# An encoder layer in which two FFN heads and the last tile are put in written order

## The chip, the cores and the metric

The kernel runs on one core of a Trainium2 chip. The metric is device time in microseconds (us) of one execution. The engines named below are TensorE (PE in the rows; its weight loads are PEld), VectorE (DVE), ScalarE (ACT), GpSimd (POOL) and SyncE (SP). Each takes its instructions in order, from a queue of its own, and waits where the next one's inputs or buffers are not ready.

## The reference

One layer of a bidirectional encoder, width 1024, on 512 columns (two sequences of 256 tokens): half an FFN, a mixer of two branches, half an FFN.

```python
def swiglu(h, w_in, w_out):
    a, g = jnp.split(h @ w_in, [D_FF], axis=-1)          # D_FF = 2816
    return (jax.nn.silu(a) * g) @ w_out
...
    x = x + 0.5 * swiglu(rmsnorm(x, g_ffn1), w_ffn1_in, w_ffn1_out)
    h = rmsnorm(x, g_mix)
...
    o_a = gla_mixer(gla_q, gla_k, gla_v, gla_r, gla_lr, gla_w2_fwd, gla_b2_fwd, gla_w2_bwd, gla_b2_bwd, gla_norm)
    o_b = mlstm_mixer(ml_qk, ml_v, ml_o, ml_if, ml_conv_w, ml_conv_b, ml_b_if, ml_norm)
    merged = jax.nn.sigmoid(gate_a.astype(f32)) * o_a + jax.nn.sigmoid(gate_b.astype(f32)) * o_b
    x = x + merged.astype(x.dtype) @ w_out
    x = x + 0.5 * swiglu(rmsnorm(x, g_ffn2), w_ffn2_in, w_ffn2_out)
```

gla_mixer is a gated linear attention in both directions, with per-column decays that are summed up along the sequence; mlstm_mixer the same with scalar gates and a running maximum.

## The kernel before

x is held transposed in eight tiles of 128 x 512. Every fp32 product is made of three matmuls over split operands: high times high, high times low, low times high (names end in h and l, or hi and lo). A weight tile is loaded raw, ScalarE casts its high part, and the low part is made in one of two ways: VectorE subtracts (split2), or ScalarE writes the negated high part and a GpSimd DMA adds the raw weights to it from memory (split_dma: names wal, wbl).

An FFN begins with its **head**. first_tiles does six column tiles (ps_f1i, three a/g pairs) as x comes in, tile by tile; in the first FFN that is the start of the kernel. rms_stat makes the scale r of the norm; its matmuls are st and sp, and dg is the diagonal between. x_sums then makes, in four steps (bodies 0 to 3), the sums and differences of x tiles from which the later products are built: u, v, t, w in VectorE, four casts xch in ScalarE, four xcl in VectorE. Two pairs are done as **plain** tiles (w_plain: names f1p and f1p2, here called the first and the second plain tile, each with two banks). The remaining pairs (f1s, numbered from 5) are done in pair, by seven products of 12 matmuls of 256 columns each, over two weight buffers: a new tile's wah waits until the tile before the last has let its buffer go. gated and activate apply r, silu and the gate, and split the result for the second matrix (out_tile).

The second FFN (f2) runs the same code; its last output tile is done in last2, in two halves of 256 columns, each with its own sum of squares (sql), scale and stores.

The order of all this is set by a scheduler, but for what is marked as high priority. The mixer between comes in gla_half (vg, gA, gB, ops_g), twice, and the mLSTM gate rows (gF, gN, gR) between the two calls.

## Time and profile before

| what | value |
|---|---|
| median of 3 runs | 1207.36 us (1204.89 to 1208.26) |
| the profiled execution | 1207.96 us |
| its span in the trace | 1206.2 us |
| busy, TensorE / VectorE / ScalarE / GpSimd | 98% / 61% / 50% / 10% |
| mean DMA rate | 118 GB/s |

The times in rows count from the span's start. What lies between the span and the execution's time, 1.8 us, is outside the trace. Matmuls overlap, so the busy time of one is longer than its turn.

### The profile page before, as it was taken

What the parts mean: (1) busy time and instruction counts of PE and PEld (TensorE: products, weight loads), DVE (VectorE), ACT (ScalarE), POOL (GpSimd) and SP (SyncE); (2) the same over time, 40 slices, a digit from 0 to 9 for tenths busy, and PEclk for the clock granted to TensorE, in tenths of its full rate; (3) what the DMA queues carried; (4) which work ended last, traced back from release to release, by engine and by line L of the source; (5) the groups of instructions that cost most, each with busy time, mean ns of one, the idle gap of its engine ahead of it and who ended that gap; (6) DMA issues with size and microseconds to landing.
All of it is one profiled execution on the core that took longest, in us unless ns stands there. A gap on an engine that the chain in (4) does not pass through costs nothing.

```text
span 1206.2 us, 16870 instructions
## 1 busy us (share of the span) xinstructions
PE 1177.4 (98%) x6651; PEld 1019.8 (85%) x6651; DVE 736.0 (61%) x1127; ACT 609.0 (50%) x989; POOL 114.9 (10%) x130
## 2 busy tenths in 40 slices
PE   8999999999999998999999999999989999999996
PEld 6798899899987887888888888888879899989985
DVE  6974576567547888657573453463585467566643
ACT  6753365256536655575762332244555256336541
POOL 4100000000021004020000000013100000000011
PEclk9999999999999999999999999999989999999997
DMA  7853555356414214232253223232754356446512
GB/s 236 192 137 112 130 141 139 116 132 164 125 53 127 88 37 131 71 105 70 79 184 114 91 93 114 81 94 44 184 141 130 101 134 156 132 119 154 139 46 70
DMA packets 57952, 141.88 MB, mean 118 GB/s; under 512 B 5320, under 2 KB 19656, under 8 KB 57872
## 3 DMA queue, kind: packets, MB, share of 16 engines
q1 hardware_dynamic: 47904, 110.38, 29.4%
q0 software_dynamic: 8160, 28.06, 13.4%
q10 hardware_dynamic: 1808, 2.36, 0.6%
q8 instruction: 52, 0.85, 0.3%
q14 instruction: 28, 0.23, 0.1%
HBM read 135.51 MB, written 2.11 MB: 114 GB/s over the span
## 4 chain that ended last, share of the span: by engine, by line
PE 89%; DVE 5%; DMA 2%; issue 2%; ACT 1%; SPq 1%; POOL 0%; POOLq 0%; DVEq 0%
PE psy_f L318 16%; PE psq_f L318 8%; PE psz_f L318 4%; PE ps_f1o L203 3%; PE ps_f1o L204 3%; PE ps_f1o L202 3%; PE ps_f2o L203 3%; PE ps_f2o L202 3%; PE ps_f2o L204 3%; PE ps_f2i L258 3%; PE pt_ga L545 2%; PE pt_ga L543 2%; PE pt_ga L544 2%; PE pt_gb L545 2%; PE pt_gb L543 2%; PE pt_gb L544 2%
## 5 line engine op out<-in xcount | busy, mean ns | idle before, releaser
L318 PE MATMUL psy_f<-xch_f,wal_f1s 128*128 128x256 f32 x204 | 57.3, 281 | 0.0
L318 PE MATMUL psy_f<-xcl_f,wah_f1s 128*128 128x256 f32 x204 | 57.2, 281 | 0.0
L318 PE MATMUL psy_f<-xch_f,wah_f2s 128*128 128x256 f32 x204 | 57.2, 281 | 0.0
L318 PE MATMUL psy_f<-xcl_f,wah_f2s 128*128 128x256 f32 x204 | 57.2, 281 | 0.0
L318 PE MATMUL psy_f<-xch_f,wal_f2s 128*128 128x256 f32 x204 | 57.2, 280 | 0.0
L318 PE MATMUL psy_f<-xch_f,wah_f1s 128*128 128x256 f32 x204 | 57.2, 281 | 0.0
L543 PE MATMUL pt_ga<-whi_ga,xh_m 128*128 128x512 f32 x128 | 50.7, 396 | 0.0
L545 PE MATMUL pt_ga<-whi_ga,xl_m 128*128 128x512 f32 x128 | 50.7, 396 | 0.0
L545 PE MATMUL pt_gb<-whi_gb,xl_m 128*128 128x512 f32 x128 | 50.5, 396 | 0.0
L544 PE MATMUL pt_ga<-wlo_ga,xh_m 128*128 128x512 f32 x128 | 50.4, 394 | 0.0
L543 PE MATMUL pt_gb<-whi_gb,xh_m 128*128 128x512 f32 x128 | 50.4, 394 | 0.0
L544 PE MATMUL pt_gb<-wlo_gb,xh_m 128*128 128x512 f32 x128 | 50.4, 394 | 0.0
L94 DVE TENSOR_TENSOR wlo_ga<-raw_ga,whi_ga 128x1024 fp32r<-128x1024 f32 x16 | 19.6, 1224 | 46.0 <-ACT whi_ga L93 46.0
L404 DVE SCALAR_TENSOR_TENSOR x<-ps_f2o,x 128x512 f32<-128x512 f32 x23 | 15.8, 689 | 41.6 <-PE ps_f2o L204 41.6
L93 ACT CAST whi_gb<-raw_gb 128x1024 fp32r<-128x1024 f32 x16 | 16.8, 1048 | 45.7 <-PE pt_ga L545 29.5
L94 DVE TENSOR_TENSOR wlo_gb<-raw_gb,whi_gb 128x1024 fp32r<-128x1024 f32 x16 | 19.6, 1222 | 32.7 <-ACT whi_gb L93 32.6
L318 PEld LDWEIGHTS psy_f<-xch_f,wah_f1s 128*128 128x128 f32 x204 | 38.4, 189 | 0.1
L318 PEld LDWEIGHTS psy_f<-xcl_f,wah_f2s 128*128 128x128 f32 x204 | 38.4, 188 | 0.1
L318 PEld LDWEIGHTS psy_f<-xcl_f,wah_f1s 128*128 128x128 f32 x204 | 38.4, 188 | 0.1
L318 PEld LDWEIGHTS psy_f<-xch_f,wal_f1s 128*128 128x128 f32 x204 | 38.5, 189 | 0.0
L318 PEld LDWEIGHTS psy_f<-xch_f,wah_f2s 128*128 128x128 f32 x204 | 38.3, 188 | 0.1
L318 PEld LDWEIGHTS psy_f<-xch_f,wal_f2s 128*128 128x128 f32 x204 | 38.4, 188 | 0.0
(1155 smaller groups left out, 4039.1 us busy)
## 6 DMA issues: line engine op xcount, KB each, us to landing
raw_f1s<-in_w_f SPq DMA_DIRECT2D x17, 512.0 KB, 3.7
wal_f1s<-in_w_f POOLq DMA_DIRECT2D x17, 512.0 KB, 5.5
raw_f2s<-in_w_f SPq DMA_DIRECT2D x17, 512.0 KB, 3.7
wal_f2s<-in_w_f POOLq DMA_DIRECT2D x17, 512.0 KB, 5.7
raw_ga<-in_w_tm SPq DMA_DIRECT2D x16, 512.0 KB, 3.6
raw_gb<-in_w_tm SPq DMA_DIRECT2D x16, 512.0 KB, 3.6
sum_f1s<-in_w_f SPq DMA_DIRECT2D x17, 256.0 KB, 3.3
raw_f1s<-in_w_f SPq DMA_DIRECT2D x17, 256.0 KB, 4.0
```

The lines of the kernel that those rows point to most:

```text
L93: nc.scalar.copy(hi[:, :width], raw[:, :width])
L94: nc.vector.tensor_tensor(out=lo[:, :width], in0=raw[:, :width], in1=hi.bitcast(F32)[:, :width], op=ALU.subtract)
L202: nc.tensor.matmul(ps, lhsT=wh, rhs=xh, start=start, stop=False)
L203: nc.tensor.matmul(ps, lhsT=wh, rhs=xl, start=False, stop=False)
L204: nc.tensor.matmul(ps, lhsT=wl, rhs=xh, start=False, stop=stop)
L258: nc.tensor.matmul(pss[m], lhsT=w[:, f[m]], rhs=xp, start=k == n == 0, stop=k == KD - 1 and n == 2)
L318: nc.tensor.matmul(ps, lhsT=l[:, f], rhs=m, start=start and k == n == 0, stop=stop and k == 3 and n == 2, skip_group_check=True)
L404: nc.vector.scalar_tensor_tensor(out=x[i], in0=ps, scalar=0.5, in1=x[i], op0=ALU.mult, op1=ALU.add)
L543: nc.tensor.matmul(pss[t], lhsT=xh, rhs=hi[:, ws], start=k == 0, stop=False)
L544: nc.tensor.matmul(pss[t], lhsT=xh, rhs=lo[:, ws], start=False, stop=False)
L545: nc.tensor.matmul(pss[t], lhsT=xl, rhs=hi[:, ws], start=False, stop=k == KD - 1)
```

## The change

There are four parts. At the start the first raw weights come in two halves over the queues of ScalarE and SyncE, and the parameters pt by ScalarE's queue instead of GpSimd's; the first xh is made by VectorE; a ScalarE activation stands early; there are 14 warm matmuls for 10. The head of each FFN gets a block in which VectorE and ScalarE keep the order of the code; the code in it is rearranged, and tile 0's split is cut in two. The second call of gla_half moves ahead of the scans of the mLSTM gates. last2 gets a written order on TensorE, VectorE and ScalarE. rms_cols and spread are each cut into two functions (rms_sum and diag, broadcast) with the same instructions; that part of the diff is left out.

```diff
@@ -117,15 +117,20 @@
     NF = 6
     raw1 = [(w_raw, w_sum)[kp % 2](f"first{kp}").rearrange("p a b -> p (a b)").rearrange("p (i m f) -> p i m f", i=2, m=NF)
             for kp in range(4)]
-    nc.scalar.dma_start(x[0], xT[0:P, :])
-    nc.gpsimd.dma_start(pt, par)
     for k in range(KD):
-        if k:
-            nc.sync.dma_start(x[k], xT[k * P:(k + 1) * P, :])
-        nc.sync.dma_start(raw1[k // 2][:, k % 2], w_f1[0:NF, :, k * P:(k + 1) * P].rearrange("m p f -> p m f"))
+        nc.sync.dma_start(x[k], xT[k * P:(k + 1) * P, :])
+        for n in ((range(0, 3), range(3, NF)) if k == 0 else (range(NF),)):
+            (nc.scalar if k == n[0] == 0 else nc.sync).dma_start(
+                raw1[k // 2][:, k % 2, n[0]:n[-1] + 1],
+                w_f1[n[0]:n[-1] + 1, :, k * P:(k + 1) * P].rearrange("m p f -> p m f"))
+        if k == 0:
+            nc.scalar.dma_start(pt, par)
+
+    act0 = cp.tile([P, 1], F32, name="act0")
+    nc.scalar.activation(act0, ones[:, 0:1], AF.Copy, scale=2.0)
 
     warm = scp("warm", (P, P))
-    for _ in range(10):
+    for _ in range(14):
         nc.tensor.matmul(warm, lhsT=ones, rhs=ones, start=True, stop=True)
     eps = cp.tile([P, 1], F32, name="eps")
     nc.gpsimd.memset(eps, EPS)
...
@@ -184,7 +199,10 @@
     def split_x(k, gcol, sq, name):
         hi = slab(f"xh_{name}{k}", F32R)
         lo = slab(f"xl_{name}{k}", F32R)
-        nc.scalar.activation(hi, x[k], AF.Copy, scale=col(gcol + k))
+        if name == "a" and k == 0:
+            nc.vector.tensor_scalar(out=hi, in0=x[k], scalar1=col(gcol + k), scalar2=None, op0=ALU.mult)
+        else:
+            nc.scalar.activation(hi, x[k], AF.Copy, scale=col(gcol + k))
         nc.vector.scalar_tensor_tensor(out=lo, in0=x[k], scalar=col(gcol + k), in1=hi.bitcast(F32),
                                        op0=ALU.mult, op1=ALU.subtract)
         add_sq(k, sq, name)
@@ -242,7 +260,10 @@
                 whi, wlo = (t.rearrange("p a b -> p (a b)")[:, i * NF * P:(i + 1) * NF * P]
                             for t in wide) if kp else (t.rearrange("p a b -> p (a b)")[:, :NF * P]
                                                        for t in w_pair("wb", 2, f"{name}{k}"))
-                if kp < dma_from:
+                if k == 0:
+                    for h in (slice(0, 3 * P), slice(3 * P, NF * P)):
+                        split2(whi[:, h], wlo[:, h], raw[:, i, h])
+                elif kp < dma_from:
                     split2(whi, wlo, raw[:, i])
                 else:
                     split_dma(whi, wlo, raw[:, i], raw[:, i])
@@ -432,9 +453,6 @@
             nc.vector.tensor_tensor(out=g, in0=b, in1=r, op=ALU.mult)
             act_of[j] = t, g
 
-        def act(j):
-            act_of[j] = activate(*act_of[j], f"{name}{j}")
-
         def plain(pss, w):
             for ps, (hi, lo) in zip(pss, w):
                 for k in range(KD):
@@ -443,25 +461,29 @@
 
         top = NP - 1
         steps = x_sums(gcol, r, name)
-        for _ in range(3):
+        with tc.manual_schedule(engines={nc.vector.engine, nc.scalar.engine}):
             next(steps)
-        w_p = w_plain(w_a, NP, f"{name}p")
-        next(steps)
-        gated(top, pss[2 * top], pss[2 * top + 1])
-        xc += next(steps)
-        plain(banks[0], w_p)
-        w_p = w_plain(w_a, NP + 1, f"{name}p2")
-        gated(0, pss[0], pss[1])
-        nxt = units[0][0]()
-        banks.append([acc(f"ps_{name}p{n}", True) for n in range(2, 4)])
-        plain(banks[1], w_p)
-        gated(1, pss[2], pss[3])
-        for j in range(NP):
-            act(j)
-        for j in (NP, NP + 1):
-            gated(j, *banks[j - NP])
-            act(j)
-        hs += [act_of[j] for j in range(NP + 2)]
+            next(steps)
+            w_p = w_plain(w_a, NP, f"{name}p")
+            next(steps)
+            next(steps)
+            gated(top, pss[2 * top], pss[2 * top + 1])
+            w_p2 = w_plain(w_a, NP + 1, f"{name}p2")
+            xc += next(steps)
+            gated(0, pss[0], pss[1])
+            plain(banks[0], w_p)
+            nxt = units[0][0]()
+            gated(1, pss[2], pss[3])
+            banks.append([acc(f"ps_{name}p{n}", True) for n in range(2, 4)])
+            plain(banks[1], w_p2)
+            for js in (range(NP), range(NP, NP + 2)):
+                for j in js:
+                    if j >= NP:
+                        gated(j, *banks[j - NP])
+                    nc.vector.tensor_tensor(out=act_of[j][0], in0=act_of[j][1], in1=act_of[j][0], op=ALU.mult)
+                for j in js:
+                    hs.append((slab(f"{name}{j}hh", F32R), slab(f"{name}{j}hl", F32R)))
+                    split2(*hs[j], act_of[j][0])
         for n, (_, run) in enumerate(units):
             cur, nxt = nxt, units[n + 1][0]() if n + 1 < len(units) else None
             run(cur)
@@ -696,6 +718,8 @@
     gN2 = grow("gN2")
     nc.vector.tensor_scalar(out=gI, in0=ss[64:72, :], scalar1=pt[64:72, C_BG:C_BG + 1], scalar2=None, op0=ALU.add)
     neg_softplus(gM, gL, ss[96:104, :], pt[96:104, C_BG:C_BG + 1])
+    gla_half(1)
+
     for c in range(4):
         s = slice(c * P, (c + 1) * P)
         nc.vector.tensor_tensor_scan(out=gF[:, s], data0=gM[:, s], data1=gL[:, s], initial=0.0,
@@ -744,7 +768,6 @@
     d_nm = dp.tile([8, T], F32, name="d_nm")
     nc.gpsimd.dma_start(d_nm, gN)
 
-    gla_half(1)
 
     cc_ps = scp("cc_ps", (P, 4, 24))
     for t in range(4):
@@ -935,16 +958,22 @@
         i = KD - 1
         sql = tmp("sql")
         n = len(hs)
-        for half in range(2):
-            cs = slice(half * SEQ, (half + 1) * SEQ)
-            ps = acc(f"ps_f2l{half}")[:, :SEQ]
-            for k in range(n):
+        cut = [slice(0, SEQ), slice(SEQ, T)]
+        pss = [acc(f"ps_f2l{half}")[:, :SEQ] for half in range(2)]
+
+        def mms(half, ks):
+            for k in ks:
                 f = slice(k * P, (k + 1) * P)
-                mm3(ps, hi[:, f], lo[:, f], hs[k][0][:, cs], hs[k][1][:, cs], k == 0, k == n - 1)
-            nc.vector.scalar_tensor_tensor(out=x[i][:, cs], in0=ps, scalar=0.5, in1=x[i][:, cs],
+                mm3(pss[half], hi[:, f], lo[:, f], hs[k][0][:, cut[half]], hs[k][1][:, cut[half]], k == 0, k == n - 1)
+
+        def final(half):
+            cs = cut[half]
+            nc.vector.scalar_tensor_tensor(out=x[i][:, cs], in0=pss[half], scalar=0.5, in1=x[i][:, cs],
                                            op0=ALU.mult, op1=ALU.add)
             nc.vector.tensor_tensor(out=sql[:, cs], in0=x[i][:, cs], in1=x[i][:, cs], op=ALU.mult)
-            rf = spread(rms_cols([sq_of("f"), sql], (2 * half, 2 * half + 1), f"f{half}"), f"f{half}").unsqueeze(1)
+
+        def scaled(half, rf):
+            cs, rf = cut[half], rf.unsqueeze(1)
             for n_ in range(KD // 2):
                 y = tmp(f"y{n_}{half}", (P, 2, SEQ))
                 xs = xg[half, n_]
@@ -955,6 +984,24 @@
                     nc.vector.scalar_tensor_tensor(out=y[:, 1:2, :], in0=x[i][:, cs].unsqueeze(1),
                                                    scalar=col(C_GF + i), in1=rf, op0=ALU.mult, op1=ALU.mult)
                 (nc.sync if n_ % 2 else nc.scalar).dma_start(out3[n_, :, :, cs], y)
+
+        with tc.manual_schedule(engines={nc.tensor.engine, nc.vector.engine, nc.scalar.engine}):
+            mms(0, range(n))
+            final(0)
+            mms(1, range(n // 2 + 1))
+            st = [rms_sum([sq_of("f"), sql], (0, 1), "f0")]
+            mms(1, range(n // 2 + 1, n))
+            rc = [small(f"rc_f{half}", 2) for half in range(2)]
+            rsqrt(rc[0], st[0], 1.0 / D, "f0")
+            final(1)
+            dg = [diag(rc[0], "f0")]
+            st.append(rms_sum([sq_of("f"), sql], (2, 3), "f1"))
+            rf = [broadcast(dg[0], "f0")]
+            rsqrt(rc[1], st[1], 1.0 / D, "f1")
+            dg.append(diag(rc[1], "f1"))
+            rf.append(broadcast(dg[1], "f1"))
+            for half in range(2):
+                scaled(half, rf[half])
 
     ffn(w_f2, w_o2, lambda k: xs2[k], raw2, 1, C_G2, sq_of("b"), "f2", done2, last2)
     last_stage.close()
```

ScalarE's queue in the head of the first FFN, before (f1p with wah_446, wal_447 is the first plain tile, with 569 and 570 already the second; xch 403 to 439 belong to bodies 0 and 1, 467 to 479 to body 2):

```order
L223 CAST xch_f_431<-xv_f_420 128x512
L228 CAST wbh_f1p_569<-sum_f1p_561 128x1024
L223 CAST xch_f_435<-xt_f_421 128x512
L229 ACTIVATE wal_f1p_447<-raw_f1p 128x1024
L223 CAST xch_f_439<-xw_f_422 128x512
L228 CAST wah_f1p_446<-raw_f1p 128x1024
L223 CAST xch_f_467<-xu_f_457 128x256
L229 ACTIVATE wbl_f1p_570<-sum_f1p_561 128x1024
L223 CAST xch_f_471<-xv_f_458 128x512
L223 CAST xch_f_475<-xt_f_459 128x512
L223 CAST xch_f_479<-xw_f_460 128x512
L431 ACT_TABLE_LOAD
```

and now, at the same place:

```order
L246 CAST wah_f1p_433<-raw_f1p 128x1024
L247 ACTIVATE wal_f1p_434<-raw_f1p 128x1024
L246 CAST wbh_f1p_439<-sum_f1p 128x1024
L247 ACTIVATE wbl_f1p_440<-sum_f1p 128x1024
L241 CAST xch_f_414<-xu_f_444 128x256
L241 CAST xch_f_456<-xv_f_445 128x512
L241 CAST xch_f_460<-xt_f_446 128x512
L241 CAST xch_f_464<-xw_f_447 128x512
L241 CAST xch_f_478<-xu_f_468 128x256
L241 CAST xch_f_482<-xv_f_469 128x512
L241 CAST xch_f_486<-xt_f_470 128x512
L241 CAST xch_f_490<-xw_f_471 128x512
```

The first plain tile's four casts now stand ahead of the casts of bodies 1 and 2, and none of the second plain tile's stands ahead of the table load.

TensorE's queue behind the second plain tile of the first FFN, before (psy 707 and psz 708 are tile 5, wah 584 its weights):

```order
L318 MATMUL psz_f_708<-xcl_f_501,wah_f1s_584 128x256
L318 MATMUL psz_f_708<-xch_f_500,wal_f1s_585 128x256
L318 MATMUL psy_f_707<-xch_f_411,wah_f1s_584 128x256
L318 MATMUL psy_f_707<-xcl_f_412,wah_f1s_584 128x256
L318 MATMUL psy_f_707<-xch_f_411,wal_f1s_585 128x256
L318 MATMUL psy_f_707<-xch_f_435,wah_f1s_584 128x256
```

and now (tile 5 is 719, 720 and 595; tile 6 is psy 811 with weights 705 and 706):

```order
L339 MATMUL psz_f_720<-xcl_f_526,wah_f1s_595 128x256
L339 MATMUL psz_f_720<-xch_f_525,wal_f1s_596 128x256
L339 MATMUL psy_f_811<-xch_f_414,wah_f1s_705 128x256
L339 MATMUL psy_f_811<-xcl_f_415,wah_f1s_705 128x256
L339 MATMUL psy_f_811<-xch_f_414,wal_f1s_706 128x256
L339 MATMUL psy_f_811<-xch_f_414,wah_f1s_705 128x256
```

Behind tile 5's psz, tile 6's first product now follows (and its psz) where tile 5's next product stood; XT2 and XT1 of tile 5 come later, one right behind the other.

VectorE's queue at the last tile, before (sp 10818 is half 0's scale; v, rc, s and dg 10862 to 10871 make that of half 1):

```order
L152 SCALAR_TENSOR_TENSOR s_f_10808<-s_f_10808,v_f_10807 128x2
L153 SCALAR_TENSOR_TENSOR rc_f_10806<-s_f_10808,rc_f_10806 128x2
L171 TENSOR_SCALAR dg_f_10815<-pt,rc_f_10806 128x128 x2
L952 TENSOR_TENSOR y_10820<-xg_10562,sp_f_10818 128x512
L952 TENSOR_TENSOR y_10823<-xg_10632,sp_f_10818 128x512
L952 TENSOR_TENSOR y_10826<-xg_10702,sp_f_10818 128x512
L954 TENSOR_TENSOR y_10829<-xg_10772,sp_f_10818 128x256
L955 SCALAR_TENSOR_TENSOR y_10829<-x_85,pt,sp_f_10818 128x256
L149 TENSOR_SCALAR v_f_10863<-st_f_10857 128x2
L150 RECIPROCAL rc_f_10862<-s_f_10864 128x2
L151 TENSOR_TENSOR s_f_10864<-rc_f_10862 128x2
L152 SCALAR_TENSOR_TENSOR s_f_10864<-s_f_10864,v_f_10863 128x2
```

and now (half 0's scale is sp 10867; 10848 to 10877 make half 1's):

```order
L971 SCALAR_TENSOR_TENSOR x_85<-ps_f2l_10795,x_85 128x256
L973 TENSOR_TENSOR sql<-x_85 128x256
L179 TENSOR_SCALAR dg_f_10859<-pt,rc_f_10847 128x128 x2
L154 TENSOR_SCALAR v_f_10869<-st_f_10862 128x2
L155 RECIPROCAL rc_f_10848<-s_f_10870 128x2
L156 TENSOR_TENSOR s_f_10870<-rc_f_10848 128x2
L157 SCALAR_TENSOR_TENSOR s_f_10870<-s_f_10870,v_f_10869 128x2
L158 SCALAR_TENSOR_TENSOR rc_f_10848<-s_f_10870,rc_f_10848 128x2
L179 TENSOR_SCALAR dg_f_10877<-pt,rc_f_10848 128x128 x2
L981 TENSOR_TENSOR y_10882<-xg_10579,sp_f_10867 128x512
L981 TENSOR_TENSOR y_10885<-xg_10649,sp_f_10867 128x512
L981 TENSOR_TENSOR y_10888<-xg_10719,sp_f_10867 128x512
```

The second scale is now made before the first multiplication by the first.

## Rows read from the trace of the kernel before

**Rows 1.** The page, part 4: the chain that ended last, by engine.

```profile
PE 89%; DVE 5%; DMA 2%; issue 2%; ACT 1%; SPq 1%; POOL 0%; POOLq 0%; DVEq 0%
```

**Rows 2.** Timeline, TensorE, rows with idle time; columns: start, us, work, [idle, releaser].

```profile
8.14 1.34 PE L258 MATMUL ps_f1i<-xh_a,wbh_f1i 128*128 128x512 f32 x4 [2.51 <-ACT wbh_f1i L223]
...
27.94 1.10 PE L173 MATMUL ps_f1p<-dg_f,ones 128*128 128x512 f32 x2 [1.46 <-DVE dg_f L171]
...
60.54 0.50 PE L204 MATMUL ps_f1p<-xh_a,wal_f1p 128*128 128x512 f32 x1 [1.76 <-DMA wal_f1p<-in_w_f]
...
454.28 0.50 PE L544 MATMUL pt_vg<-wlo_vg,xh_m 128*128 128x512 f32 x1 [2.59 <-DVE wlo_vg L94]
...
464.27 0.50 PE L544 MATMUL pt_vg<-wlo_vg,xh_m 128*128 128x512 f32 x1 [1.25 <-DVE wlo_vg L94]
...
884.51 0.80 PE L204 MATMUL ps_f2p<-xh_b,wal_f2p 128*128 128x512 f32 x1 [4.93 <-DMA wal_f2p<-in_w_f]
...
1193.18 0.95 PE L173 MATMUL sp_f<-dg_f,ones 128*128 128x256 f32 x2 [2.02 <-DVE dg_f L171]
...
1198.22 1.22 PE L173 MATMUL sp_f<-dg_f,ones 128*128 128x256 f32 x2 [2.59 <-DVE dg_f L171]
```

**Rows 3.** Windows: length, busy time by engine (started), granted clock (PEclk), DMA share, GB/s.

```profile
450.00:466.00 16.00, 12.16 (x64) 9.89 (x63) 16.00 (x35) 10.65 (x20) 2.73 (x2) 1.00 0.21 57
...
884.50:890.00 5.50, 5.49 (x14) 4.32 (x15) 4.46 (x6) 0.63 (x1) 0.00 (x0) 0.53 0.93 262
...
890.00:895.00 5.00, 5.00 (x23) 4.07 (x22) 2.64 (x4) 2.96 (x5) 0.00 (x0) 1.00 0.00 0
```

**Rows 4.** Timeline, head of the first FFN; last line: the tile wal_f1p, its transfers.

```profile
38.62 0.41 PE L258 MATMUL ps_f1i<-xh_a,wah_f1i 128*128 128x512 f32 x1
...
45.90 1.28 ACT L431 ACT_TABLE_LOAD   x1 [1.59 <-DVE f1t L430]
...
51.36 0.84 POOL L230 DMA_DIRECT2D wal_f1p<-in_w_f  x1 [7.46 <-ACT wal_f1p L229]
...
DMA to landing us min/median/max: 5.5/7.3/9.1
```

**Rows 5.** Timeline, head of the second FFN, the same places.

```profile
859.77 1.06 ACT L228 CAST wah_f2p<-raw_f2p 128x1024 fp32r<-128x1024 f32 x1 [0.39 <-PE ps_f2i L258]
...
869.99 0.69 DVE L302 TENSOR_TENSOR sum_f2s<-sum_f2s,raw_f2s 128x512 f32<-128x512 f32 x1 [10.90 <-DMA raw_f2s<-in_w_f]
...
876.85 0.85 POOL L230 DMA_DIRECT2D wal_f2p<-in_w_f  x1 [16.31 <-ACT wal_f2p L229]
```

**Rows 6.** Window in psy work; timeline behind the second plain tile; wal_f1s, 50 to 90 us.

```profile
200.00:210.00 10.00, 10.00 (x87) 10.00 (x86) 4.80 (x8) 4.53 (x9) 0.00 (x0) 1.00 0.43 137
...
65.72 1.05 ACT L299 CAST wah_f1s<-raw_f1s 128x1024 fp32r<-128x1024 f32 x1 [3.82 <-PE ps_f1p L203]
...
68.54 0.85 POOL L301 DMA_DIRECT2D wal_f1s<-in_w_f  x1 [12.85 <-PE ps_f1p L203]
...
78.60 1.05 ACT L299 CAST wah_f1s<-raw_f1s 128x1024 fp32r<-128x1024 f32 x1 [0.99 <-PE psy_f L318]
...
81.17 0.85 POOL L301 DMA_DIRECT2D wal_f1s<-in_w_f  x1 [11.78 <-ACT wal_f1s L300]
...
DMA to landing us min/median/max: 5.7/5.8/7.5
```

**Rows 7.** Timeline, VectorE: first and last of 34 rows of the mLSTM gates.

```profile
431.96 0.41 DVE L701 TENSOR_TENSOR_SCAN gF<-gM,gL 8x128 f32<-8x128 f32 x1 [4.93 <-ACT gL L528]
...
447.03 0.41 DVE L742 TENSOR_SCALAR gN<-gN 8x512 f32<-8x512 f32 x1
```

**Rows 8.** Timeline, VectorE, last tile; DMA view of 1194 to 1206.2 in 40 slices.

```profile
1194.24 1.88 DVE L952 TENSOR_TENSOR y<-xg,sp_f 128x512 f32<-128x512 f32 x3 [1.11 <-PE sp_f L173]
...
1199.48 1.88 DVE L952 TENSOR_TENSOR y<-xg,sp_f 128x512 f32<-128x512 f32 x3 [1.31 <-PE sp_f L173]
...
GB/s 0 0 0 0 0 0 0 0 310 340 330 326 356 340 356 337 343 333 40 0 0 0 0 283 323 350 323 363 307 363 343 336 353 93 0 0 0 0 0 0
```

More of the change, by code (lines that the diff above doesn't have):

```diff
@@ L153, in rsqrt, with rms_sum @@
         nc.vector.scalar_tensor_tensor(out=dst, in0=s, scalar=1.5, in1=dst, op0=ALU.add, op1=ALU.mult)
-    def rms_cols(parts, cs, name, bank=None):
+    def rms_sum(parts, cs, name, bank=None):
         ps = scp(f"st_{name}", (P, len(cs))) if bank is None else bank[:, :len(cs)]
@@ L161, in rms_cols, with diag @@
                                  start=n == 0, stop=n == len(parts) - 1)
+        return ps
+    def rms_cols(parts, cs, name, bank=None):
         r = small(f"rc_{name}", len(cs))
-        rsqrt(r, ps, 1.0 / D, name)
+        rsqrt(r, rms_sum(parts, cs, name, bank), 1.0 / D, name)
         return r
-    def spread(r, name, bank=None):
+    def diag(r, name):
         n = r.shape[-1]
@@ L171, in spread, with broadcast @@
             nc.vector.tensor_scalar(out=dg[:, c, :], in0=ident, scalar1=r[:, c:c + 1], scalar2=None, op0=ALU.mult)
-        ps = scp(f"sp_{name}", (P, n * P)) if bank is None else bank
+        return dg
+    def broadcast(dg, name, bank=None):
+        ps = scp(f"sp_{name}", (P, dg.shape[1] * P)) if bank is None else bank
         nc.tensor.matmul(ps, lhsT=ones, rhs=dg.rearrange("p c t -> p (c t)"), start=True, stop=True)
         return ps
+    def spread(r, name, bank=None):
+        return broadcast(diag(r, name), name, bank)
     def rms_stat(sq, name, banks=(None, None)):
```

## The prediction, made before the changed kernel had run

> **What bounds the kernel now.** I read the page first: the chain that ended last [rows 1]. TensorE carries 89% of it, so an edit elsewhere counts only where it makes a TensorE gap longer or shorter, or moves the end behind its last matmul. The second view is therefore TensorE's timeline, cut to the rows with idle time in brackets [rows 2]: eight gaps, 19.1 us together, each with its releaser. They are what this change can win. The third view is the granted clock by stretch [rows 3]: the 450 to 466 stretch holds gaps of 2.59 and 1.25 us, and the clock stays 1.00 (2.4 GHz). Behind the 4.93 us gap it is 0.53 (near 1.2 GHz), with 14 matmuls started in 5.5 us where the next 5 us start 23. 5.5 us would have held 25, so 11 are lost, at 0.22 us each: such a fall costs 2.4 us. The last views are the timelines of ScalarE, VectorE and GpSimd at the FFN heads [rows 4 to 6], in the gates [rows 7] and at the end [rows 8].
>
> The profiled execution took 1207.96 us, 0.6 above the median of the three runs; the sum is made against 1207.96 and 0.6 comes off last. A measurement can tell 0.3%, 3.6 us, from no change.
>
> **Start: 0.** The first weights come in halves and xh of tile 0 moves to VectorE, so the 2.51 us gap should shrink. But TensorE then reaches the statistics matmuls earlier, where it waits for the sum of squares and VectorE's dg_f (the 1.46 us gap, [rows 2]), and those come from the later tiles' loads, which are as late as before. What is left moves the first head earlier, and that one waits for weights anyway. Bounds -0.8 to +0.8. The early table load and four more warm matmuls lie in time in which their engines wait.
>
> **First head, up to the second plain tile.** ScalarE's queue is now as written. wah_f1p stands ahead of the casts of bodies 1 and 2, and it cannot begin before TensorE has used tile 5's weights, 38.6, or 38.9 with the lag (its buffer is that of the first tiles). Before, both bodies' casts ran ahead of it. From 38.9 the chain is: four 1024-wide casts, about 1.0 us each after 1.06 in [rows 5], to 42.7; body 1's casts, one of 256 and three of 512, 1.9 together by halving that, to 44.6; VectorE's last xcl of body 1 (0.69 a 512-wide operation, [rows 5]), body 2's two 512-wide and four 256-wide ones, 3.4, to 48.1; ScalarE's last cast of body 2 and VectorE's remaining three xcl, to 50.1; f1t, 50.8; table load 1.28 [rows 4] and silu, 52.7; wah_f1p2 and wal_f1p2, 54.7; GpSimd issues at 55.0. Before it issued at 51.36 [rows 4]. The transfer took 9.1 us there; in the second FFN it landed 7.6 after its issue (876.85 to 884.51, [rows 2, 5]). With the middle, 8.2, TensorE goes on at 63.2 instead of 60.54; the two matmuls of the fourth bank that now stand ahead of the wait take back 0.47 (two at 0.23): **+2.2**, bounds 1.3 to 3.2. The gap becomes about 3 us. Between start and end of the run no row has a gap between 2.59 (clock stays) and 4.93 (falls), so I put half of 2.4: **+1.2**, bounds 0 and 2.4.
>
> **Second head, the same place.** Before, VectorE stood 10.9 us at an addition that waits for a later tile's load, with f2t behind it [rows 5]; written order puts f2t ahead. What takes the place of that wait is the chain above, from 859.77: 16.1 us to the issue, 875.9, against 876.85. With 7.6 us it lands at 883.5, 1.0 earlier, and 0.47 as above: **-1.4**, bounds -3.5 to 0. The gap is still 3.5 us, so half of the clock's price comes back: **-1.2**, bounds -2.4 and 0.
>
> **Both heads, behind the second plain tile.** Here nothing waits now. TensorE's new order sends the whole X11 and X21 products of tile 6 ahead of tile 5's second group, and that brings three waits. Let T be the end of the third bank (65.7, where wah_f1s could start, [rows 6]). Tile 6 is needed at T plus 22 matmuls of 512 and 24 of 256, 5.1 + 2.8 = 7.9, and two more, 8.1; a 256-wide one takes 0.115 by 87 in 10 us [rows 6]. wal_f1s is issued 2.8 after T before, 3.3 with a 1024 cast in place of a 512 one ahead of it; its transfers landed after 5.7 to 7.5, median 5.8 [rows 6]: T + 9.1. Wait 1.0. Next, the products XT2 and XT1 of tile 5 stand back to back with ScalarE's copy of the bank between: 0.6 (a 256-wide copy and two handovers). Third, tile 7: it takes tile 5's buffer, free at XT1's end. Before, that release was at 78.60 and the issue at 81.17, and with 5.8 it landed 8.4 after the release. Before, 36 more matmuls of tile 6 (4.1 us) stood between XT1 and that need, and covered it; now 53 are left, 6.1 us, so TensorE waits 2.3. Together 3.9, say **+4.0 a head, +8.0**. Bounds 2 (the copy hidden, and each transfer 0.7 earlier) and 6 (7.5 for each transfer).
>
> The price hangs on the transfer's length. The Trainium skill (DMA: Bandwidth & Descriptors, "Anatomy of one DMA — SWDGE (gpsimd) path") fits 2.0 us plus bytes over 436 GB/s, by which these 512 KB would land in an estimated 3.2 us. The rows have 5.5 to 9.1 and decide; by the page's figure the first and third of these waits would shrink to the 1.2 us that wah_f1s needs, and the terms behind the second plain tile would be 1.8 a head instead of 4.0.
>
> **Gates behind both halves.** The scans and row operations of the mLSTM gates, 34 rows on VectorE between 431.96 and 447.4 [rows 7], leave the time in which wlo_vg is late. The 2.59 and 1.25 us waits go: -3.8. Next late are the four sets of gA and gB, which filled TensorE between vg's matmuls and now stand behind each other; VectorE empties each bank with two operations of 0.69, and I take one such pair as exposed: 1.4 back. Two more table loads (1.28 each) come on ScalarE, which waits there. Behind it, the row stores and their loads are later, ahead of mLSTM work that TensorE reaches some 50 us on. **-2.4**, bounds -3.8 and +1.
>
> **Last tile.** Before, the second half's sum of squares and scale stand behind the first half's stores: y of half 1 starts at 1199.48, after half 0's at 1194.24 [rows 8]. Now VectorE has both scales first: half 0 starts about where it did, behind the second rsqrt, and half 1 follows after 2.6 us of half 0's operations, at 1196.8, 2.7 earlier. But the eight stores are 2 MB, and they move at some 340 GB/s, first at 1196.5 and last at 1204.4, with a hole of 1.6 us between (slices of 0.31 us, [rows 8]). Without the hole they end at 1202.7. **-1.7**, bounds -2.7 (VectorE's gain whole) and -1.
>
> **Sum.** 0 + 2.2 + 1.2 - 1.4 - 1.2 + 8.0 - 2.4 - 1.7 = +4.7: 1212.7, less 0.6, **1212.1 us**.
>
> **Rivals.** *Faster:* the accumulating transfers land in 5.5, the shortest row [rows 4], since the plain loads beside them are spread otherwise. It decides from the point where the second head's gap stays under 2.59 us and the clock holds. First head 60.5 and 0.47 less: -0.5; second 881.4 less 0.47, and 2.4: -6.0; behind it 0.7 + 0.6 + 2.0 a head: +6.6; gates -3.8, end -1.7: -5.4, or 1202 us. For it: 5.5 and 5.7 stand in the rows; against it: the two at this very place took 7.6 and 9.1. *No change:* the three waits behind the second plain tile overlap (TensorE's first wait gives the later loads time) and cost 2.0 a head: +0.7, or 1208 us. Against it: the third is counted from XT1's own end, which moves with the others. *Slower still:* the clock falls in the first head and is not won back in the second, 6 a head, gates +1: 2.2 + 2.4 - 1.4 + 12 + 1 - 1.7 = +14.5, or 1222 us. *The written order does not bite:* if VectorE and ScalarE had had this order anyway, the heads would stay and only gates and end count: -4.1, 1203; the two queues do differ, so little is left for it.
>
> By the page's 3.2 us the second head's gap would be gone, and the time would be an estimated 1198; all rows of these transfers are longer, so I give that 0.03.
>
> **How the numbers follow.** Forecast 0.48, no change 0.22, faster rival 0.15, the page's case 0.03, order without effect 0.02, slower still 0.10. Of the forecast's own spread (1207 to 1217) a fifth lies within 3.6 us of before. That gives faster 0.20, same 0.31, slower 0.49. The range of 8 in 10 reaches from 1201, under the faster rival, to 1219, short of the slowest.
>
> **What would show it.** In the profile after: the second wal_f1p is issued on GpSimd's queue at about 55 and that of f2 within 1 us of before; VectorE's 10.9 us wait is gone; rows with idle time appear in psy of tiles 6 and 7 of either FFN, 1 to 2.5 us each, their releasers the transfer wal and ScalarE's copy; the vg waits are gone, with short ones at gA or ops_g; y of half 1 follows half 0 at once. I am wrong if the psy waits are not there (transfers faster, or TensorE late for another reason), if the wal of f2 is issued by 872, or if the gate rows, now later, hold up the mLSTM part.

## The result and the profile after

The changed kernel took 1219.12 us (median of 4 runs, 1217.92 to 1221.33) against 1207.6 (4 runs, 1204.89 to 1208.26): a ratio of 1.0102, 95% interval 1.0081 to 1.0123. It is 11.5 us slower. Slower was forecast, at +4.7; the time lies just outside the range (1219).

The profiled execution took 1217.92 us, its span 1216.1, 9.9 above the span before. The page gives TensorE's busy time and share:

```profile
PE 1183.6 (97%) x6659; PEld 1023.4 (84%) x6659; DVE 735.2 (60%) x1130; ACT 611.5 (50%) x993; POOL 110.4 (9%) x129
```

6.2 us of the 9.9 are in busy time (1177.4 before), though the change adds only four small matmul calls (eight records) at the start. So TensorE did not only wait longer, it also ran slower in places.

The timeline of TensorE, rows with idle time in the two heads (those of before are in [rows 2]):

```profile
47.43 0.50 PE L222 MATMUL ps_f1p<-xh_a,wal_f1p 128*128 128x512 f32 x1 [1.58 <-DMA wal_f1p<-in_w_f]
...
61.54 0.50 PE L222 MATMUL ps_f1p<-xh_a,wal_f1p 128*128 128x512 f32 x1 [2.24 <-DMA wal_f1p<-in_w_f]
...
79.90 0.55 PE L339 MATMUL psy_f<-xch_f,wal_f1s 128*128 128x256 f32 x1 [3.24 <-DMA wal_f1s<-in_w_f]
...
89.03 0.39 PE L339 MATMUL psy_f<-xch_f,wah_f1s 128*128 128x256 f32 x1 [0.52 <-ACT f1u L402]
...
91.73 0.38 PE L339 MATMUL psy_f<-xch_f,wah_f1s 128*128 128x256 f32 x1 [1.02 <-ACT wah_f1s L320]
...
878.11 0.50 PE L222 MATMUL ps_f2p<-xh_b,wal_f2p 128*128 128x512 f32 x1 [1.65 <-DMA wal_f2p<-in_w_f]
...
892.35 0.80 PE L222 MATMUL ps_f2p<-xh_b,wal_f2p 128*128 128x512 f32 x1 [2.37 <-DMA wal_f2p<-in_w_f]
...
909.41 0.55 PE L339 MATMUL psy_f<-xch_f,wal_f2s 128*128 128x256 f32 x1 [2.01 <-DMA wal_f2s<-in_w_f]
...
918.50 0.39 PE L339 MATMUL psy_f<-xch_f,wah_f2s 128*128 128x256 f32 x1 [0.52 <-ACT f2u L402]
...
921.20 0.38 PE L339 MATMUL psy_f<-xch_f,wah_f2s 128*128 128x256 f32 x1 [1.02 <-ACT wah_f2s L320]
```

Each head has two waits up to the second plain tile (the first of them new) and three behind it, where before had none. What ends those three is a GpSimd transfer (wal), ScalarE's copy f1u and ScalarE's cast wah; the forecast had named the first two. The granted clock by window (columns as in [rows 3]):

```profile
62.80:66.20 3.40, 3.40 (x10) 2.62 (x9) 2.16 (x3) 0.30 (x1) 0.00 (x0) 0.50 1.07 205
...
79.90:83.40 3.50, 3.50 (x17) 3.50 (x18) 3.50 (x6) 1.52 (x5) 0.00 (x0) 0.51 0.66 224
...
83.40:88.00 4.60, 4.60 (x42) 4.60 (x41) 3.28 (x5) 0.93 (x2) 0.00 (x0) 1.00 0.09 36
...
455.00:475.00 20.00, 20.00 (x88) 16.17 (x87) 19.73 (x40) 14.07 (x24) 0.00 (x0) 1.00 0.24 79
```

Behind the 2.24 us wait, and again behind the 3.24 us one, the clock is 0.50 (near 1.2 GHz) for about 3.4 us: 17 matmuls of 256 columns start in 3.5 us, where the next 4.6 us start 42. 3.5 us would have held 32; 15 lost at 0.11 are 1.6 us. The second FFN has the same pair, at 892.3 and 909.3. Before, the stretch from 12.5 to 880 had no fall. The last window shows TensorE busy throughout 455 to 475 in the mixer, where the two vg waits stood before.

GpSimd's queue in the first head, with the landing times of wal_f1s between 50 and 110 us ([rows 4, 6] before):

```profile
53.47 0.86 POOL L248 DMA_DIRECT2D wal_f1p<-in_w_f  x1 [11.34 <-ACT wal_f1p L247]
...
71.60 0.87 POOL L322 DMA_DIRECT2D wal_f1s<-in_w_f  x1 [9.40 <-DVE wbl_f1s L242]
...
93.21 0.87 POOL L322 DMA_DIRECT2D wal_f1s<-in_w_f  x1 [20.74 <-ACT wal_f1s L321]
...
DMA to landing us min/median/max: 5.4/5.9/8.2
```

and in the second head (wal_f2s between 870 and 930 us):

```profile
884.17 0.87 POOL L248 DMA_DIRECT2D wal_f2p<-in_w_f  x1 [11.34 <-ACT wal_f2p L247]
...
902.33 0.87 POOL L322 DMA_DIRECT2D wal_f2s<-in_w_f  x1 [9.44 <-DVE wbl_f2s L242]
...
DMA to landing us min/median/max: 5.4/5.8/6.9
```

Measured at the same instruction in both traces, the delay against before grows like this:

| place | delay, us | step | forecast |
|---|---|---|---|
| first scale of the first FFN | -1.8 | start | 0 |
| first plain tile's wal, first FFN | 0.0 | what the start won is waited out | 0 |
| first psy, first FFN | +2.1 | first head | +3.4 |
| first matmul of the second matrix | +9.9 | behind the second plain tile: +7.8 | +4.0 |
| first matmul of the second FFN | +8.0 | gates: -1.9 | -2.4 |
| first psy, second FFN | +6.5 | second head: -1.5 | -2.6 |
| first matmul of its second matrix | +13.2 | behind the second plain tile: +6.7 | +4.0 |
| end of the span | +9.9 | last tile: -3.3 | -1.7 |

### The profile page after: what moved, and what is told of

Same layout as the page of the kernel before. It is cut to its first block, busy times and chain, and to the rows that moved or that the text cites. A ratio compares the mean times of both kernels' runs of the same rounds, so it can differ in the third digit from the quotient of the medians.

```text
span 1216.1 us, 16906 instructions
## 1 busy us (share of the span) xinstructions
PE 1183.6 (97%) x6659; PEld 1023.4 (84%) x6659; DVE 735.2 (60%) x1130; ACT 611.5 (50%) x993; POOL 110.4 (9%) x129
## 5 line engine op out<-in xcount | busy, mean ns | idle before, releaser
L339 PEld LDWEIGHTS psy_f<-xch_f,wal_f2s 128*128 128x128 f32 x204 | 38.9, 191 | 2.6 <-issue 2.2
L339 PEld LDWEIGHTS psy_f<-xch_f,wah_f1s 128*128 128x128 f32 x204 | 38.9, 191 | 2.3 <-ACT wah_f1s L320 1.2
L339 PEld LDWEIGHTS psy_f<-xch_f,wah_f2s 128*128 128x128 f32 x204 | 38.9, 191 | 2.3 <-ACT wah_f2s L320 1.2
```

The source lines that it names most:

```text
L339: nc.tensor.matmul(ps, lhsT=l[:, f], rhs=m, start=start and k == n == 0, stop=stop and k == 3 and n == 2, skip_group_check=True)
```

## The experiments

Each kernel was timed beside the kernel before on the same chip, and the ratio is to that. The changed kernel itself was at 1.0102. Differences between medians of two changed kernels are across chips in part, and good to 1 or 2 us.

**e1: the heads undone.** The kernel before with the other three parts.

```diff
-        with tc.manual_schedule(engines={nc.vector.engine, nc.scalar.engine}):
...
+        for _ in range(3):
+            next(steps)
+        w_p = w_plain(w_a, NP, f"{name}p")
...
```

> The changed kernel with both FFN heads as they were before; start, gates and last tile stay changed. Theory A (the heads cost the time, the other parts bring what the two traces show: gates 1.9, end 3.3, start 1.8 if nothing eats it): 1200.5 to 1202.5 us, 5 to 7 below before. Rival B (the start makes the heads collide, the heads' order itself costs little): 1207 or above.

Measured: 1202.99 us, 0.996 (0.9945 to 0.9975). Theory A holds, half a microsecond outside its range: without the heads the change is a gain of 4.7 us, so the heads cost 16. TensorE's timeline shows where most of the start's gain goes: a wait of 1.25 us at the first plain tile, which the kernel before did not have. The second plain tile waits about as before (1.64 for 1.76), and the second head's gap is back in full.

```profile
47.14 0.50 PE L222 MATMUL ps_f1p<-xh_a,wal_f1p 128*128 128x512 f32 x1 [1.25 <-DMA wal_f1p<-in_w_f]
...
60.18 0.50 PE L222 MATMUL ps_f1p<-xh_a,wal_f1p 128*128 128x512 f32 x1 [1.64 <-DMA wal_f1p<-in_w_f]
...
882.49 0.80 PE L222 MATMUL ps_f2p<-xh_b,wal_f2p 128*128 128x512 f32 x1 [5.42 <-DMA wal_f2p<-in_w_f]
```

**e2: the heads alone.** The kernel before with the written order of the heads.

```diff
+        with tc.manual_schedule(engines={nc.vector.engine, nc.scalar.engine}):
+            next(steps)
+            next(steps)
+            w_p = w_plain(w_a, NP, f"{name}p")
...
```

> The kernel before with the written order of both heads alone. Theory A, from the shifts between the two traces (+2.1 up to the second plain tile and +7.8 behind it in the first FFN, -1.5 and +6.6 in the second): +15, 1222 to 1223 us. Rival B (the earlier start is what makes the heads late): under 1215.

Measured: 1228.3 us, 1.016 (1.014 to 1.018). It is worse than theory A said, by 5 us, and rival B is out. So the parts do not add up: 20.6 lost here and 4.7 won in e1 would make 16, and the changed kernel lost 11.5. In the profiled execution (1224.32, the fastest of the four) the second plain tile's wait in the first FFN is 4.71 us instead of 2.24, and the second head's tile 6 waits 3.65 instead of 2.01. The first of these transfers is issued 14.1 us behind the first plain tile's, as in the changed kernel, but landed after 10.4 us instead of 8.0; that of tile 6 landed after 8.1 instead of 6.9. Why they took longer is not shown.

```profile
66.12 0.80 PE L204 MATMUL ps_f1p<-xh_a,wal_f1p 128*128 128x512 f32 x1 [4.71 <-DMA wal_f1p<-in_w_f]
...
84.43 0.36 PE L318 MATMUL psy_f<-xch_f,wal_f1s 128*128 128x256 f32 x1 [3.31 <-DMA wal_f1s<-in_w_f]
...
914.23 0.36 PE L318 MATMUL psy_f<-xch_f,wal_f2s 128*128 128x256 f32 x1 [3.65 <-DMA wal_f2s<-in_w_f]
```

**e3: TensorE's order put back.** The changed kernel with tile 5's products ahead of tile 6's.

```diff
-        for n, (_, run) in enumerate(units):
+        with tc.manual_schedule(engines={nc.tensor.engine}):
+            for n, (_, run) in enumerate(units[:3]):
+                cur, nxt = nxt, units[n + 1][0]()
+                run(cur)
+        for n, (_, run) in enumerate(units[3:], 3):
```

> The changed kernel with TensorE's order written too for the first three units behind the plain tiles: tile 5's second products stand ahead of tile 6 again, as before. Theory A1 (TensorE's new order and the transfer that it runs into are the cost): the waits behind the second plain tile and the half clock behind them go in both heads, about -13, 1206 us. Theory A2 (the copy of tile 5's bank in ScalarE stands behind the silu of the plain tiles, which wait for VectorE, so tile 5 is late too): a first wait of some 3 us stays, with the releaser ScalarE, and only the two later waits go, about -5, 1214 us.

Measured: 1215.97 us, 1.0062 (1.0045 to 1.0079), 3.2 below the changed kernel. Theory A1 falls and A2 holds, with 3.2 of its 5 us: the first wait stays, longer than in the changed kernel, with another releaser, and the two later ones go.

```profile
79.94 0.58 PE L339 MATMUL psy_f<-xch_f,wah_f1s 128*128 128x256 f32 x1 [3.92 <-ACT f1m L395]
```

The copy f1m of tile 5's bank stands in ScalarE's queue behind the silu of the fourth pair, and that waits for VectorE's gate f1t. In front of this gate VectorE has the products and splits of the first three pairs, which are in the written block, and tile 6's sums and first split, which are not and which the scheduler put between. In the changed kernel VectorE's timeline shows the first of tile 6's rows, the last of them ahead of the gate, and the gate:

```profile
64.04 0.69 DVE L323 TENSOR_TENSOR sum_f1s<-sum_f1s,raw_f1s 128x512 f32<-128x512 f32 x1 [4.43 <-DMA sum_f1s<-in_w_f]
...
76.33 1.75 DVE L242 TENSOR_TENSOR wal_f1s<-sum_f1s,wah_f1s 128x1536 fp32r<-128x1536 f32 x1
...
78.59 0.68 DVE L451 TENSOR_TENSOR f1t<-ps_f1p,r_f 128x512 f32<-128x512 f32 x1
```

So TensorE's new order is no slip: the bank of tile 5 is not free before 79.9 in either order, and the scheduler filled in tile 6. The first row shows something more: VectorE stands 4.43 us (4.15 in the second head) at tile 6's first sum, which waits for a load that SyncE issued at 55.10, and the rest of tile 5's sums and the gate are behind it. That is the fault which the written order was to remove, a gate behind a row that waits for a load, at another place. No run takes this wait out, so its share is not shown.

**e4: tile 6 without its transfer.** VectorE subtracts.

```diff
+        if j == 6:
+            split2(ah[:, 0:2], al[:, 0:2], raw[:, 0:2])
+        else:
...
```

> The changed kernel with the low part of tile 6's first weights made by a VectorE subtraction in both heads, so that this transfer and its wait are gone; TensorE's order of tiles 5 and 6 stays. Theory A1 (the transfer of tile 6 alone holds TensorE, 3.2 and 2.0 us, and the clock falls behind it): both waits and both half-clock stretches go, -8, 1211 us. Theory A2 (VectorE's row behind is next): a wait of about 1.3 us for VectorE's f1t at psq takes its place, no fall of the clock, -6, 1213 us. Rival: VectorE's added work makes up for it, 1218 or more.

Measured: 1211.28 us, 1.0032 (1.0021 to 1.0042), 7.8 below the changed kernel: A1's size. A2's wait is there all the same, 1.71 us for VectorE's gate f1t. From 26.5 to 1190 us the clock is full, even behind the 2.34 us wait at the second plain tile, which stands ahead of the edit and is as long as in the changed kernel. So A1 has the size, but not as the sum of waits that went; more on this behind e10.

```profile
61.95 0.50 PE L222 MATMUL ps_f1p<-xh_a,wal_f1p 128*128 128x512 f32 x1 [2.34 <-DMA wal_f1p<-in_w_f]
...
79.79 0.36 PE L342 MATMUL psq_f<-xch_f,wah_f1s 128*128 128x256 f32 x1 [1.71 <-DVE f1t L454]
...
60.00:66.00 6.00, 4.05 (x18) 3.30 (x19) 1.56 (x3) 1.44 (x2) 0.87 (x1) 1.00 1.07 218
...
76.00:86.00 10.00, 7.49 (x61) 7.11 (x60) 10.00 (x16) 4.30 (x8) 0.00 (x0) 1.00 0.36 107
```

**e5: the written block ended early.** The rows of finished pairs (silu, gate, split) are left to the scheduler.

```diff
-            for js in (range(NP), range(NP, NP + 2)):
+        for js in (range(NP), range(NP, NP + 2)):
...
```

> The changed kernel with the written block of each head ended behind the second plain tile: silu, gates and splits of the finished pairs are left to the scheduler, as before. Theory A (the written order of those rows on VectorE and ScalarE delays the rows that free tile 5's banks and the transfer of tile 6): most of what is lost behind the second plain tile comes back, 3 to 5 a head, 1210 to 1213 us. Rival B (the loss comes from where the weights are issued, ahead of these rows): within 2 us of the changed kernel, 1217 to 1220.

Measured: 1211.98 us, 1.0038 (1.0024 to 1.0053), 7.1 below the changed kernel: the time is theory A's. The wait at tile 6 is gone in the first FFN and 0.45 us in the second. What stays is a wait of 2.16 us for tile 7's transfer (2.15 in the second), and the second plain tile is issued as late as in the changed kernel, at 53.44. The profiled execution was one of the slower of ten (1215.38, of 1209.3 to 1216.6) and shows only 2.5 us of the 7.1:

```profile
95.76 0.39 PE L339 MATMUL psy_f<-xch_f,wal_f1s 128*128 128x256 f32 x1 [2.16 <-DMA wal_f1s<-in_w_f]
...
53.44 0.86 POOL L248 DMA_DIRECT2D wal_f1p<-in_w_f  x1 [11.34 <-ACT wal_f1p L247]
```

**e6: a short block, in the kernel of e1.** Only what made the second head late is written: bodies 0 and 1, the first plain tile's casts, body 2, the top gate, the second plain tile's casts.

```diff
-        for _ in range(3):
+        with tc.manual_schedule(engines={nc.vector.engine, nc.scalar.engine}):
+            for _ in range(3):
+                next(steps)
+            w_p = w_plain(w_a, NP, f"{name}p")
             next(steps)
...
+            gated(top, pss[2 * top], pss[2 * top + 1])
+            w_p2 = w_plain(w_a, NP + 1, f"{name}p2")
         xc += next(steps)
...
```

> The kernel of e1 (start, gates, last tile) with a short written block in each head: bodies 0 and 1, then the first plain tile's casts, body 2, the top pair's gate, the second plain tile's casts; all behind is left to the scheduler. Theory A (the useful part of written order is that the gate no longer stands behind the 10.9 us wait for a load, and the harm is in the rest): the second head's gap of 5.4 us shrinks under 1 and its half clock goes, 6 to 7 us below e1's 1203, 1196 to 1198 us. Rival B (any written order turns TensorE's later order round and brings the waits of tiles 6 and 7): 1203 or above.

Measured: 1196.39 us, 0.9905 (0.9888 to 0.9921): faster than both kernels, 11.2 us below before and some 23 below the changed one. Theory A. The second plain tile's transfer is issued at 48.38, 3 us before its time in the kernel before, and at 867.55, 9 us before, of which 3.7 come from the parts ahead. Each head keeps one wait, at the first plain tile, and the clock is full in both stretches:

```profile
47.39 0.50 PE L222 MATMUL ps_f1p<-xh_a,wal_f1p 128*128 128x512 f32 x1 [1.70 <-DMA wal_f1p<-in_w_f]
...
866.45 0.50 PE L222 MATMUL ps_f2p<-xh_b,wal_f2p 128*128 128x512 f32 x1 [1.68 <-DMA wal_f2p<-in_w_f]
...
48.38 0.86 POOL L248 DMA_DIRECT2D wal_f1p<-in_w_f  x1 [6.39 <-ACT wal_f1p L247]
...
867.55 0.86 POOL L248 DMA_DIRECT2D wal_f2p<-in_w_f  x1 [6.40 <-ACT wal_f2p L247]
...
60.00:100.00 40.00, 40.00 (x293) 37.64 (x292) 27.08 (x37) 21.96 (x35) 1.73 (x2) 1.00 0.54 140
...
860.00:900.00 40.00, 38.32 (x214) 32.91 (x213) 33.00 (x49) 27.77 (x38) 5.19 (x6) 1.00 0.76 179
```

**e7: one line moved in the changed kernel.** Body 1 is written ahead of the first plain tile's casts; the rest of the block stays.

```diff
-            next(steps)
-            next(steps)
+            for _ in range(3):
+                next(steps)
             w_p = w_plain(w_a, NP, f"{name}p")
             next(steps)
-            next(steps)
```

> The changed kernel with body 1 written ahead of the first plain tile's casts, the block otherwise whole. Theory A (the chain from tile 5's last matmul over both bodies is what issues the second plain tile late): its transfers are issued 3 to 4 us earlier in both heads, the gaps of 2.2 and 2.4 us there go with their half clock, 6 to 8 below the changed kernel, 1211 to 1213 us. Rival B (what is won there is waited out behind the second plain tile, whose loads are paced by buffers): within 2 us of the changed kernel.

Measured: 1207.47 us, 0.9994 (0.9981 to 1.0006), 11.7 below the changed kernel, more than theory A's 6 to 8. The transfer is issued 5 us earlier (48.50 for 53.47), and the second plain tile waits in neither head. The wait at tile 6 is still there:

```profile
48.50 0.86 POOL L248 DMA_DIRECT2D wal_f1p<-in_w_f  x1 [6.39 <-ACT wal_f1p L247]
...
75.35 0.38 PE L339 MATMUL psy_f<-xch_f,wal_f1s 128*128 128x256 f32 x1 [2.96 <-DMA wal_f1s<-in_w_f]
```

Some 12 of the 16 us that the heads cost thus hung on one place in the written order: the first plain tile's four casts, which cannot begin before TensorE is done with the first tiles' weights, written ahead of body 1, which can. The block of this kernel is that of e6 carried on to the end of the head, so what is written behind it costs 11 us against e6, and the whole block still 4.5 against e1.

**e8: tile 7's loads held back.** One element of each target is written from tile 5's copy, so the loads wait for it.

```diff
+        if j == 7:
+            for dst in (raw[:, 0, 0:1], raw[:, 2, 0:1], sm[:, 0, 0:1]):
+                nc.gpsimd.tensor_copy(out=dst, in_=m_of[-1][:, 0:1])
...
+            m_of.append(m)
```

> The changed kernel, in which the loads of tile 7's raw weights wait until tile 5's first bank has been copied (a one-element copy from that copy into each of the loads' targets, on GpSimd), in both heads. In the changed kernel they are issued at 69.6 to 72.0, beside the transfer of tile 6's wal (71.6, landed 8.3 later). Theory A1 (these loads are what lengthens it): it lands after 5.4 to 6, the wait at tile 6 shrinks from 3.2 and 2.0 to about 1 us in both heads, and with it a half-clock stretch; 3 to 6 below the changed kernel, 1213 to 1216 us, if tile 7's weights are still in time; where they are not, the gain is taken back there. Rival (the transfer is long for another reason): it still takes 7 to 8 us.

Measured: 1212.66 us, 1.0034 (1.0022 to 1.0046), 6.5 below the changed kernel. A1 for the transfer: tile 6's lands after 5.8 us instead of 8.2 (5.7 instead of 6.9 in the second FFN), and its wait is 0.83 us. Tile 7 is late for it (1.99 us), as the expectation allowed, and the second plain tile waits 3.68 us in this trace, so that TensorE stands idle as long as in the changed kernel; where the 6.5 us come from follows behind e10.

```profile
72.79 0.87 POOL L327 DMA_DIRECT2D wal_f1s<-in_w_f  x1 [10.41 <-ACT wal_f1s L326]
...
78.69 0.36 PE L344 MATMUL psy_f<-xch_f,wal_f1s 128*128 128x256 f32 x1 [0.83 <-DMA wal_f1s<-in_w_f]
...
96.83 0.39 PE L344 MATMUL psy_f<-xch_f,wal_f1s 128*128 128x256 f32 x1 [1.99 <-DMA wal_f1s<-in_w_f]
...
DMA to landing us min/median/max: 5.7/5.8/6.4
```

In the changed kernel SyncE issues those loads right beside it; the 14.53 us row is two issues of sum_f1s, the second standing at the head of the queue until its buffer is free:

```profile
55.10 14.53 SPq L317 DMA_DIRECT2D sum_f1s<-in_w_f  x2
...
71.63 0.33 SPq L316 DMA_DIRECT2D raw_f1s<-in_w_f  x1
...
72.01 0.43 SPq L318 DMA_DIRECT2D raw_f1s<-in_w_f  x1
```

**e9: the wait filled with matmuls, in the kernel of e3.** 24 matmuls into a bank that is begun anew behind them.

```diff
+            if j == NP + 2:
+                q = acc(f"psq_{name}{j}", True)
+                for _ in range(2):
+                    product(q, w[1], xc[X21], True, True)
...
```

> The kernel of e3 with 24 matmuls of 256 columns more on TensorE, ahead of the wait for tile 5's copy in both heads; they write a bank that is begun anew after them, so the output is the same. The waits there are 3.9 us, the added work 2.8 us, so it fits in. Theory C (the half-clock stretch behind such a wait, 6.8 us long in e3, is a cost of its own, 2.9 us a head): the clock stays full behind it and the time is 4 to 6 us below e3's 1216, 1210 to 1212, with more work on TensorE. Rival (the clock falls for the earlier gaps anyway): 1215 to 1217.

Measured: 1219.82 us, 1.0095 (1.008 to 1.011), 3.9 above e3. This one went wrong as an experiment: the bank that I chose is freed by the same late gate, so the added matmuls did not fill the wait but stood behind it.

```profile
79.25 0.36 PE L339 MATMUL psq_f<-xch_f,wah_f1s 128*128 128x256 f32 x1 [3.00 <-DVE f1t L456]
```

It says nothing on the clock. It does show that another of tile 5's banks, psq, is held by VectorE's gate too.

**e10: e6 without the change of the start.**

```diff
-    for _ in range(14):
+    for _ in range(10):
...
-                if k == 0:
-                    for h in (slice(0, 3 * P), slice(3 * P, NF * P)):
...
```

> The kernel of e6 with the start as it was before (first loads, first xh, ten warm matmuls, tile 0 split whole). In the changed kernel the start's 1.8 us are there at the first scale and gone at the first plain tile, which waits 1.6 us for its transfer. Theory A (a start's gain is kept as far as the head's chain begins with it and nothing behind it waits for something else; in e6 1.9 to 2.0 stay): 1.5 to 2.5 above e6's 1196.4, 1198 to 1199 us. Rival (the first head's loads set the time whatever the start does): within 0.7 of e6.

Measured: 1200.7 us, 0.9929 (0.9915 to 0.9943); e6 was at 0.9905. The start is worth 2.4 thousandths, 2.9 us by the ratios, since the two ran on different chips; that is a little above theory A's 2.5. In e6 what the start wins is kept: the first plain tile's wal is used at 47.39 for 50.61 here, with the same wait ahead of it (1.70 and 1.66). The changed kernel keeps it as well when it is set against e2, which has the heads without the start (47.43 for 49.54). In e1 the new wait at the first plain tile takes most of it.

**Idle time and clock.** The traces of the changed kernel and of four experiments on it tell the two apart. The idle time is that of TensorE's rows in the two heads; the half clock is the time in the heads in which TensorE worked at a granted clock of 0.50.

| kernel | profiled execution, us | idle in both heads, us | at half clock, us |
|---|---|---|---|
| changed | 1217.92 | 16.4 | 13.5 |
| e4 | 1210.35 | 15.6 | 0 |
| e5 | 1215.38 | 14.4 | 13.0 |
| e7 | 1208.78 | 10.6 | 6.8 |
| e8 | 1212.66 | 16.4 | 2.8 |

A stretch of 3.4 us at half clock costs 1.6, so the difference in clock is worth 6.3 us in e4 and 5.0 in e8. That is nearly all of the 7.6 and 5.3 us by which these executions are faster; their waits moved to other places and hardly shrank. In e7 idle time gives 5.8 and the clock 3.1 of 9.1. Two of the four falls of the changed kernel stand at the second plain tiles, ahead of what e4 and e8 edit. In e4 the clock held at both, in e8 at one, behind waits about as long (2.34, 2.00 and 1.95 us); why is not shown. It is not the luck of one execution: the mean granted clock lies between 0.988 and 0.991 in the four executions of the changed kernel, 0.990 and 0.995 in the ten of e4, 0.992 and 0.995 in the seven of e8.

## Why the forecast was too small

*Start, 0:* right as a number. Of its two reasons the first failed: the first scale was to come no earlier than before, and came 1.8 us earlier. The second held: this gain is waited out at the first plain tile, which I had not named as the place.

*First head, +3.4 forecast, +2.1 measured.* The chain through ScalarE and VectorE was right in kind and in length: 16.4 us from its first cast to the issue, 16.1 forecast. The issue came at 53.47, not 55.0, since the start had moved that cast from 38.9 to 37.07, which I had set to nothing here:

```profile
37.07 1.05 ACT L246 CAST wah_f1p<-raw_f1p 128x1024 fp32r<-128x1024 f32 x1 [4.91 <-issue]
```

The transfer took 8.0 us, where I had 8.2 (the middle of 9.1 and 7.6 is 8.35; the slip is 0.15 us). The clock fell in full, 1.6 us, where I had half of 2.4.

*Second head, -2.6 forecast, -1.5 measured.* The issue came at 884.17, 876.2 without the delay up to there, for 875.9 forecast. The 10.9 us wait for a load in VectorE's queue is gone from this place (one of 4.15 us comes further on, as told under e3). What I left out is a wait of 1.65 us at the first plain tile: its transfer is issued 2.4 us later than before (870.07, less the delay of 8.0, for 859.68), since its casts come one behind the other once tile 5 is done. The clock still fell behind the second wait, for 3.4 us instead of the 5.2 that followed the gap before, so some 0.8 of the 1.2 came back.

*Behind the second plain tile, +4.0 a head forecast, +7.8 and +6.7 measured: this is the step that failed.* Its three waits came, at the tiles named: 3.24, 0.52 and 1.02 us in the first FFN, 2.01, 0.52 and 1.02 in the second, against 1.0, 0.6 and 2.3. Two things were mis-sized. First the transfer of tile 6: I took the median of 5.8 and it lasted 8.2 and 6.9, because the loads of tile 7, which before were issued at 60.6, now stand in SyncE's queue until 69.6 and go beside it; e8 parts them and it lands in 5.8 and 5.7. I had asked what the written order does to ScalarE, VectorE and TensorE, and not what it does to SyncE's loads, whose buffers those engines free. Second, and larger, I priced a fall of the clock at the two second plain tiles and put it at nothing here, where the waits are as long; it fell in both heads, 1.6 us each. The three waits together are 0.9 us more than forecast in the first head and 0.4 less in the second, so the clock is the greater part of what can be named of the 3.8 and 2.7 us that were missing. The rest, 1.3 and 1.5, is in what each wait costs beyond its row and in waits under 0.4 us. An estimate: idle time counts from the end of the last matmul, whose row lasts 0.39 us while its turn is 0.12, so three waits cost some 0.8 more than their rows.

The third wait was smaller than forecast and another: at tile 7 TensorE waits 1.02 us for ScalarE's cast wah, and the transfer wal, which I had priced, landed at 98.60 and is waited for by less than 0.4. In e5 there is a wait for that transfer, 2.16 and 2.15 us, close to the 2.3 of the forecast.

*The cause that I gave for these waits,* TensorE's new order, was only half of it: e3 puts the order back and keeps a wait of 3.92, because tile 5's copy is late by the written order of ScalarE and VectorE. e5 leaves the rows of the finished pairs to the scheduler, and the first wait goes: their order holds tile 5's bank. VectorE's wait for tile 6's load shrinks there too, from 4.43 to 2.79 us, and no run parts the two. What these waits cost in time goes by the table behind e10: in e5's trace 2.0 us of idle time went, and its falls of the clock stayed.

*Gates, -2.4 forecast, -1.9 measured:* right in size. The vg waits are gone, but what comes back is not at gA and gB, where I had put 1.4: it is waits of 0.44 us, for a gate row (gR), and 1.37 us later in the mixer. That the size fits is partly luck.

*Last tile, -1.7 forecast, -3.3 measured.* I took the stores as the floor at 340 GB/s. They moved without a hole and faster, at 369 to 394 in the full slices, and the first half's sums had moved into the matmuls, which brought both scales forward:

```profile
1207.28 1.88 DVE L981 TENSOR_TENSOR y<-xg,sp_f 128x512 f32<-128x512 f32 x3
...
1209.80 1.88 DVE L981 TENSOR_TENSOR y<-xg,sp_f 128x512 f32<-128x512 f32 x3
...
GB/s 0 0 0 0 0 0 0 0 0 0 0 0 0 0 0 0 0 0 306 388 375 385 388 378 382 394 372 385 391 378 382 394 369 388 369 6 0 0 0 0
```

The rival "slower still" (1222, with 6 a head) came nearest. Of its conditions the fall of the clock in the first head came, and the long transfer at tile 6; its loss of 1 us at the gates did not.

## What to carry to other kernels

Written order on two engines should hold only the rows whose order is known to matter: here a short block up to one gate and the casts behind it was worth 6.6 us over the scheduler's order (e6 against e1), the same block carried on to the end of the head cost 4.5 (e7 against e1), and with four casts ahead of rows that could have run, 16 (the changed kernel). A block orders only its own rows: the scheduler put tile 6's sum, which waits for a load, between them. Before writing an instruction into a queue that waits for another engine, put ahead of it what can run without that wait. Follow each moved reader to the buffer that it frees: the next load waits for it, and where that load then lands decides which transfer it slows. And when a run is faster, ask whether waiting shrank or the clock stayed up: in e4 and e8 it was nearly all the clock.
